# Prompt attention: the value products of a tile as two double bursts in its fifth and seventh slots, in place of four bursts in every other slot

## The chip, the cores and the metric

The kernel runs on one core of a Trainium2 chip. The metric is device microseconds of one execution, median of three runs. The core's engines work side by side and wait for each other at semaphores: TensorE (PE, matmuls and transposes into PSUM), VectorE (DVE), ScalarE (ACT), GpSimd (POOL) and the queue of SyncE (SP) that issues the transfers.

## The reference

A trunk of two encoder layers, applied to a prompt of 1024 positions and a sample of 256, both of width 1024. A layer normalises its input, projects it, and adds four groups of branches (attention, Fourier mixing, spatial gating, memory attention) through one output projection. The change touches the attention alone: 8 query heads, 2 key heads, 64 wide, no mask.

```python
def one_block(qblk):     # 128 queries
    s = jnp.einsum('bqkgd,bskd->bkgqs', qblk, k, preferred_element_type=jnp.float32) * scale
    p = jax.nn.softmax(s, axis=-1)
    return jnp.einsum('bkgqs,bskd->bqkgd', p.astype(v.dtype), v)
o_att = self_attention(q, k, v) * jax.nn.silu(ag)
```

## The kernel before

All matrix work is done in float32 or, split into a high and a low part, as float32r products. Per layer the stages follow each other: spatial gating, Fourier mixing, memory attention, the projections of queries, keys and values, then `attention` (lines 712 to 891), then `output`. The order of TensorE's instructions in the attention is that of the program; those of the other engines are ordered by a scheduler.

`attention` goes over ten tiles of 128 queries, eight of the prompt (t = 0 to 7, 1024 keys) and two of the sample (256 keys). A tile has eight slots, i = 0 to 7, called first to eighth here, one for each head, in the order 2, 0, 3, 1, 6, 4, 7, 5. So slots one, three, five and seven have the heads with j = 2 or 3 of their key head, and the even-numbered slots those with j = 0 or 1. In a slot TensorE gets, in this order:

- the score of the next slot's head (`score`, L761: four matmuls of 512 columns into an `s` tile of PSUM, of which there are two). VectorE takes the maximum (L764), ScalarE the exponential with its sum (L766). The score of a tile's first head is so issued in the eighth slot of the tile before; it is called the opening score.
- in slots one, three, five and seven the first entry of `todo`, work left by the tile before.
- in slots four and six the transposes of the next tile's queries (`turn_q`, L733, copied by ScalarE at L734).
- for heads with j below 2 the transposes of the slot's probabilities (`turn`, L794: two halves of four, copied by ScalarE at L799 into `pt`). Heads with j of 2 or 3 are transposed in blocks of 32 by VectorE instead (L776), and moved into `pd` by POOL and 12 transfers (L785, L787); for those heads TensorE gets nothing here.

The values of a tile come one tile late. `values(t, part, kts)` (lines 819 to 836) multiplies the values of some key tiles with the transposed probabilities and adds up in one PSUM tile `acc` of the pool `mm` (four buffers): part 0 for the heads that came through TensorE (`pt`), part 1 for the others (`pd`). A call for four key tiles is eight instructions of 256 columns, a burst; each has two records in the trace. `norm_gate` (L816) spreads the reciprocal row sums by four transposes and multiplies the gate by them (L817), and `finish` (L841, L842) multiplies the sum by the gate and stores it. `todo` (lines 881 to 886) says which of these goes into which slot: one burst in each of the slots one, three, five and seven, the gate's transposes behind the second, `finish` behind the last.

`pt` and `pd` are two of the four buffers `a16`. In the sample tiles one output product (`product`, L928, twelve matmuls of 512 columns) follows each slot. Its left operand is loaded, and converted by ScalarE (L915) and VectorE (L916), in `load_o`, into `a16` buffers that prompt attention gives back.

Of the kernel before, what the change touches and what calls it, by code (L numbers as in the profile page):

```python
# [74 lines left out]
def trunk_kernel(  # L75
# [10 lines left out]
    nc = tc.nc  # L86
# [29 lines left out]
    def mm(shape, dt=F32):  # L116
        return ps.tile(shape, dt, tag="mm", bufs=4, name=uid("mm_"))
# [594 lines left out]
    def attention(l, q_d, kT, v8, v2, ag, o_att):  # L712
# [5 lines left out]
        def load_q(t):  # L718
            if t < NT:
                raw[t] = c2([P, 8, HD])  # L720
                nc.sync.dma_start(raw[t], q_d[t])

        def prep_q(t):
            q = raw.pop(t)
            qhl = c4([P, 8, 2, HD], F32R)
            nc.scalar.copy(qhl[:, :, 0, :], q)
            nc.gpsimd.tensor_tensor(qhl[:, :, 1, :], q, fv(qhl)[:, :, 0, :], ALU.subtract)
            return qhl

        def turn_q(qhl, qT, kv):  # L730
            pt = mm([P, 4, P], F32R)
            for j in range(4):
                nc.tensor.transpose(pt[:, j, :], qhl[:, 4 * kv + j].rearrange("p a d -> p (a d)"), ident_r)  # L733
            nc.scalar.copy(qT[:, 4 * kv:4 * kv + 4], fv(pt))  # L734
# [3 lines left out]
        def open_tile(t):  # L738
            e = dict(prompt=t < 8, nk=SEQ if t < 8 else DEC, qT=c4([P, 8, P], F32R),
                     rs=st([P, 4, 2], tag="rowsum", bufs=3))  # L740
            tiles[t] = e

        def open_rest(t):
            e = tiles[t]
            if e["prompt"]:
                e["pt"] = a16([P, 8, 2, 2, P], F32)
                e["pd"] = a16([P, 4, 2, 8, 2, 32], F32)
            else:
                e["pt"] = [c4([P, 2, 4, P]) for _ in range(2)]

        def score(t, h):
            g, _ = group_of(t)
            e = tiles[t]
            nk = e["nk"]
            kv, j = h // 4, h % 4
            s = s2([P, 1024])
            for kg in ((0, 1) if g < 2 else (2,)):
                n = GROUPS[kg][1]
                c0 = GROUPS[kg][0] if g < 2 else 0
                for b in range(2):  # L760
                    nc.tensor.matmul(s[:, c0:c0 + n], e["qT"][:, h, :], kT[kg][b][:, kv, :],  # L761
                                     start=b == 0, stop=b == 1)
            nm = st([P, 1])
            nc.vector.tensor_reduce(nm, s[:, :nk], axis=AX.X, op=ALU.max, negate=True)  # L764
            p = c4([P, 1024])
            nc.scalar.activation(p[:, :nk], s[:, :nk], AF.Exp, bias=nm, accum_out=e["rs"][:, j, kv:kv + 1])  # L766
            e[h] = p

        def turn(t, h):
            e = tiles[t]  # L770
            kv, j = h // 4, h % 4
            p = e.pop(h)
            if e["prompt"] and j >= 2:
                if j == 2:
                    e["blocks"] = a8([P, 4, 8, 2, 32], F32)
                nc.vector.transpose(e["blocks"][:, :, :, j - 2].rearrange("p b k q -> p k b q"),  # L776
                                    p.rearrange("p (k b q) -> p k b q", b=4, q=32))
                if j == 3:
                    for r in range(4):
                        for a in range(4):  # L780
                            b = (a + r) % 4
                            dst = e["pd"][32 * b:32 * b + 32, a, kv].rearrange("p k j q -> p (k j q)")
                            src = e["blocks"][32 * a:32 * a + 32, b].rearrange("p k j q -> p (k j q)")
                            if r == 0:
                                nc.gpsimd.tensor_copy(dst, src)  # L785
                            else:
                                nc.sync.dma_start(dst, src)  # L787
                return
            for half in range(2 if e["prompt"] else 1):
                kn = 4 if e["prompt"] else 2  # L790
                pt = mm([P, 4, P])
                for kk in range(kn):
                    c0 = (half * 4 + kk) * P
                    nc.tensor.transpose(pt[:, kk, :], p[:, c0:c0 + P], ident)  # L794
                if e["prompt"]:
                    dst = e["pt"][:, half * 4:half * 4 + kn, kv, j, :]
                else:
                    dst = e["pt"][kv][:, :, j, :]
                nc.scalar.copy(dst, pt[:, :kn])  # L799

        def load_gate(t):
            gt = tiles[t]["gt"] = c2([P, 4, P])
            nc.sync.dma_start(gt, ag[t])

        def norm_rows(t):
            e = tiles[t]
            r = st([P, 4, 2], tag="rowsum_r", bufs=2)
            nc.vector.reciprocal(r, e["rs"])
            e["rb"] = c2([P, 4, 2, HD])
            nc.gpsimd.tensor_copy(e["rb"], r.unsqueeze(3).to_broadcast([P, 4, 2, HD]))  # L810

        def norm_gate(t):
            e = tiles[t]
            rt = mm([P, 4, P])
            for j in range(4):
                nc.tensor.transpose(rt[:, j, :], e["rb"][:, j].rearrange("p a d -> p (a d)"), ident)  # L816
            nc.vector.tensor_tensor(e["gt"], e["gt"], rt, ALU.mult)  # L817

        def values(t, part, kts):
            e = tiles[t]  # L820
            if "acc" not in e:
                e["acc"] = mm([P, 4, P])
            acc = e["acc"]
            last = e["nk"] // P - 1
            for kt in kts:
                for kv in range(2):
                    out = acc[kv * HD:(kv + 1) * HD]
                    vt = (v8 if t < 8 else v2)[:, kt, kv * HD:(kv + 1) * HD]
                    if not e["prompt"]:
                        out, src = out.rearrange("p j t -> p (j t)"), e["pt"][kv][:, kt].rearrange("p j t -> p (j t)")  # L830
                    elif part == 0:
                        out, src = out[:, 0:2].rearrange("p j t -> p (j t)"), e["pt"][:, kt, kv].rearrange("p j t -> p (j t)")
                    else:
                        out = out[:, 2:4].rearrange("p j (a q) -> p j a q", q=32)
                        src = e["pd"][:, :, kv, kt].rearrange("p a j q -> p j a q")
                    nc.tensor.matmul(out, vt, src, start=kt == 0, stop=kt == last)  # L836

        def finish(t):
            e = tiles.pop(t)
            o = c2([P, 4, P])  # L840
            nc.vector.tensor_tensor(o, e["acc"], e["gt"], ALU.mult)  # L841
            nc.sync.dma_start(o_att[:, :, t * P:(t + 1) * P], o)  # L842
# [13 lines left out]
        todo = []  # L856
        for n, (t, i, h) in enumerate(work):
            if i == 1 and t + 1 < NT:
                qhl = prep_q(t + 1)
            if i == 3 and t + 1 < NT:  # L860
                load_q(t + 2)
                open_tile(t + 1)
            if i == 4:
                load_gate(t)
            if i == 7 and t + 1 < NT:
                open_rest(t + 1)
            if n + 1 < len(work):
                score(work[n + 1][0], work[n + 1][2])
            if i % 2 == 0 and todo:
                for f in todo.pop(0):  # L870
                    f()
            if i in (3, 5) and t + 1 < NT:
                turn_q(qhl, tiles[t + 1]["qT"], (i - 3) // 2)
            turn(t, h)
            if i == 7:
                for fs in todo:
                    for f in fs:
                        f()
                norm_rows(t)
                if t < 8:  # L880
                    todo = [[lambda t=t, part=part, k=k: values(t, part, range(k, k + 4))]
                            for part in range(2) for k in range(0, 8, 4)]
                    todo[1].append(lambda t=t: norm_gate(t))
                else:
                    todo = [[lambda t=t: norm_gate(t)], [lambda t=t: values(t, 0, range(2))]]
                todo[-1].append(lambda t=t: finish(t))
            yield t, i
# [133 lines left out]
    for l in range(DEPTH):  # L1021
# [34 lines left out]
        last = l == DEPTH - 1  # L1056
        out_hT = []
        out = output(l, o_d, xin if l == 0 else xmid, xout if last else xmid, out_hT)
# [100 lines left out]
```

## Time and profile before

| | us |
|---|---|
| median of 3 runs | 2187.02 (2184.76 to 2191.01) |
| profiled execution | 2190.76 |
| its span, first to last instruction | 2189.0 |
| TensorE busy | 2140.2 (98%) |
| TensorE weight loads busy | 1832.7 (84%) |
| VectorE busy | 1122.5 (51%) |
| ScalarE busy | 853.1 (39%) |
| value products L836, busy | 127.9 in 1024 records |
| scores L761, busy | 163.5 in 576 records |

Busy time of TensorE is modelled, with matmuls overlapping in its pipeline, so one instruction's duration in a timeline is longer than the distance to the start of the next. In what follows distances from start to start are used. An idle time in square brackets in a timeline is that before the first instruction of the row, with what ended it.

### The profile page before, as it was taken

To read this page: it belongs to the slowest core of one execution; us is meant where nothing else is said; L and a number is where in the kernel's file an instruction comes from. 1 tells how busy PE (TensorE), PEld (TensorE's weight loads), DVE (VectorE), ACT (ScalarE), POOL (GpSimd) and SP (SyncE) were. 2 spreads that over 40 slices of the span, in tenths; PEclk is the share of its full clock that TensorE was granted. 3 is DMA by queue.
4 is the path that set the end of the run, shared out by engine and by line. 5 is a ranking of instruction groups with operands and counts; after the bars stand their busy time and mean duration, and the time that the engine had idled before them with its cause. 6 is when DMAs were issued, how large, how long until landed. Compare 5 with 4: busy or idle time off the path is not lost.

```text
span 2189.0 us, 33399 instructions
## 1 busy us (share of the span) xinstructions
PE 2140.2 (98%) x12872; PEld 1832.7 (84%) x12872; DVE 1122.5 (51%) x1972; ACT 853.1 (39%) x1935; POOL 324.7 (15%) x544
## 2 busy tenths in 40 slices
PE   7999999999999999999999999999999999999997
PEld 7898988888899777678888988888889877767885
DVE  5345344444574577534465343454557467752445
ACT  6133232333341577642254222233433267763121
POOL 2010000000032233100053000000003123310005
PEclk9999999999999999999999999999999999999999
DMA  4123431211212344522343120121112234452224
GB/s 176 57 98 116 140 109 63 71 61 35 77 50 89 108 113 118 149 86 88 106 143 113 58 78 32 63 86 48 50 63 69 80 101 124 112 151 82 87 106 144
DMA packets 113679, 202.55 MB, mean 93 GB/s; under 512 B 17393, under 2 KB 52593, under 8 KB 113521
## 3 DMA queue, kind: packets, MB, share of 16 engines
q1 hardware_dynamic: 113520, 200.42, 29.1%
q8 instruction: 102, 1.67, 0.3%
q14 instruction: 57, 0.46, 0.1%
HBM read 129.05 MB, written 46.14 MB: 80 GB/s over the span
## 4 chain that ended last, share of the span: by engine, by line
PE 87%; DMA 3%; DVE 3%; ACT 3%; POOL 2%; issue 2%; SPq 1%; DVEq 0%; POOLq 0%; ACTq 0%
PE mm L248 35%; PE mm L928 16%; PE mm L261 12%; PE s L761 6%; PE mm L836 5%; PE mm L794 3%; PE mm L311 2%; PE mm L327 1%; PE s L422 1%; PE s L408 1%; PE s L576 1%; PE mm L609 1%; POOL c L953 1%; PE s L217 1%; DVE c L961 1%
## 5 line engine op out<-in xcount | busy, mean ns | idle before, releaser
L248 PE MATMUL mm<-a,ws 128*128 128x512 f32 (+1 forms) x4032 | 795.1, 355 | 0.0
L248 PEld LDWEIGHTS mm<-a,ws 128*128 128x128 f32 x4032 | 663.6, 189 | 102.4 <-issue 0.5
L928 PE MATMUL mm<-ws,a 128*128 128x512 f32 x1632 | 381.4, 392 | 0.7 <-ACT c L935 0.6
L928 PEld LDWEIGHTS mm<-ws,a 128*128 128x128 f32 x1632 | 304.8, 188 | 65.3 <-issue 1.6
L261 PE MATMUL mm<-ws,a 128*128 128x256 f32 x2400 | 304.2, 287 | 0.0
L261 PEld LDWEIGHTS mm<-ws,a 128*128 128x128 f32 x2400 | 296.8, 195 | 0.5 <-DVE a L234 0.2
L764 DVE TENSOR_REDUCE st<-s 128x1 f32<-128x1024 f32 (+1 forms) x160 | 170.0, 1062 | 123.2 <-PE s L761 123.2
L273 ACT ACTIVATE c<-mm 128x512 f32<-128x512 f32 (+1 forms) x96 | 50.8, 529 | 322.7 <-PE mm L248 319.0
L766 ACT ACTIVATE c<-s,st 128x1024 f32<-128x1024 f32 (+1 forms) x160 | 159.2, 995 | 37.3 <-DVE st L764 36.5
L274 DVE SCALAR_TENSOR_TENSOR c<-c,mm 128x512 f32<-128x512 f32 (+1 forms) x96 | 57.3, 597 | 219.2 <-ACT c L273 219.2
L761 PE MATMUL s<-c,c 128*128 128x512 f32 (+1 forms) x576 | 163.5, 401 | 3.5 <-ACT c L766 2.8
L148 POOL TENSOR_SCALAR st<-st 128x1 f32<-128x1 f32 (+3 forms) x120 | 27.0, 225 | 745.7 <-DVE st L654 454.8
L166 ACT ACTIVATE ws<-wr,pre_g 128x256 fp32r<-128x256 f32 x304 | 126.6, 505 | 22.1 <-DMA wr<-in_w_in_dram 15.6
L836 PE MATMUL mm<-a,c 128*64 128x256 f32 x1024 | 127.9, 389 | 5.2 <-ACT a L799 5.2
L167 DVE SCALAR_TENSOR_TENSOR ws<-wr,pre_g,ws 128x256 fp32r<-128x256 f32 x304 | 128.7, 484 | 2.1 <-ACT ws L166 2.0
L761 PEld LDWEIGHTS s<-c,c 128*128 128x128 f32 x576 | 98.8, 189 | 35.0 <-issue 15.4
L937 DVE TENSOR_TENSOR c<-c,mm 128x512 f32<-128x512 f32 x120 | 81.1, 683 | 83.0 <-PE mm L928 82.9
L836 PEld LDWEIGHTS mm<-a,c 128*64 128x64 f32 x1024 | 68.8, 137 | 55.7 <-issue 19.7
L785 POOL COPY a<-a 32x512 f32<-32x512 f32 x128 | 80.2, 627 | 199.1 <-DVE a L776 141.7
L150 POOL TENSOR_TENSOR st<-st,mhalf 128x1 f32<-128x1 f32 (+3 forms) x120 | 99.8, 832 | 9.9
L953 POOL TENSOR_TENSOR c<-c,c 128x512 f32<-128x512 f32 x40 | 55.8, 1395 | 272.8 <-ACT c L948 272.7
L144 DVE TENSOR_TENSOR ws<-wr,ws 128x1024 fp32r<-128x1024 f32 x48 | 57.0, 1222 | 62.2 <-ACT ws L143 62.1
(121 smaller groups left out, 2286.0 us busy)
## 6 DMA issues: line engine op xcount, KB each, us to landing
wr<-in_w_in_dram SPq DMA_DIRECT2D x76, 512.0 KB, 4.1
a<-a SPq DMA_DIRECT2D x384, 64.0 KB, 2.0
wr<-in_w_out_dram SPq DMA_DIRECT2D x32, 512.0 KB, 3.9
wr<-o SPq DMA_DIRECT2D x48, 256.0 KB, 3.0
c<-in_x_prompt_dram SPq DMA_DIRECT2D x16, 512.0 KB, 6.4
o<-c SPq DMA_DIRECT2D x32, 256.0 KB, 2.0
wr<-in_w_mem_kv_dram SPq DMA_DIRECT2D x16, 512.0 KB, 4.5
q<-c SPq DMA_DIRECT2D x40, 128.0 KB, 1.7
```

Of the source, the lines that this page charges most:

```text
L150: nc.gpsimd.tensor_tensor(r, m, mhalf[:, :n], ALU.pow)
L166: nc.scalar.activation(w[:, 0, kk], raw[:, k], AF.Copy, scale=g)
L167: nc.vector.scalar_tensor_tensor(w[:, 1, kk], raw[:, k], g, fv(w)[:, 0, kk], ALU.mult, ALU.subtract)
L248: nc.tensor.matmul(acc[:, :n], w[:, a, k, c * P:(c + 1) * P], hT.t[g][b][:, k, :], start=i == 0, stop=i == 3 * KC - 1)
L261: nc.tensor.matmul(acc[:, :256], hT.t[g][a][:, k, tt * P:(tt + 1) * P], w[:, b, k, :], start=i == 0, stop=i == 3 * KC - 1)
L761: nc.tensor.matmul(s[:, c0:c0 + n], e["qT"][:, h, :], kT[kg][b][:, kv, :], start=b == 0, stop=b == 1)
L764: nc.vector.tensor_reduce(nm, s[:, :nk], axis=AX.X, op=ALU.max, negate=True)
L766: nc.scalar.activation(p[:, :nk], s[:, :nk], AF.Exp, bias=nm, accum_out=e["rs"][:, j, kv:kv + 1])
L785: nc.gpsimd.tensor_copy(dst, src)
L836: nc.tensor.matmul(out, vt, src, start=kt == 0, stop=kt == last)
L928: nc.tensor.matmul(acc, oT[g][c][:, a, tt * P:(tt + 1) * P], w[:, b, c, :], start=j == 0, stop=j == 11)
L937: nc.vector.tensor_tensor(ys, ys, acc, ALU.add)
```

## The change

The list `todo` that a prompt tile leaves for the next has an empty entry for the first slot, the gate's transposes for the third, and for the fifth and the seventh a burst of part 0 and one of part 1 for the same four key tiles. As both parts now begin in one slot and share the PSUM tile, only the first matmuls of part 0 carry the start flag, and only the last of part 1 (or of part 0 in a sample tile) the stop flag.

```diff
-                    nc.tensor.matmul(out, vt, src, start=kt == 0, stop=kt == last)
+                    nc.tensor.matmul(out, vt, src, start=kt == 0 and part == 0, stop=kt == last and part == int(e["prompt"]))
...
                 if t < 8:
-                    todo = [[lambda t=t, part=part, k=k: values(t, part, range(k, k + 4))]
-                            for part in range(2) for k in range(0, 8, 4)]
-                    todo[1].append(lambda t=t: norm_gate(t))
+                    todo = [[], [lambda t=t: norm_gate(t)]]
+                    todo += [[lambda t=t, part=part, k=k: values(t, part, range(k, k + 4)) for part in range(2)]
+                             for k in range(0, 8, 4)]
```

TensorE, first layer, second prompt tile, first to third slot. Names: `s` are scores, `mm` PSUM tiles of the other kinds, `a` the transposed probabilities. Before:

```order
L836 MATMUL mm_7406<-a_925_7073,c_698_5348 64x256 x8
L761 MATMUL s_989_7420<-c_693_5343,c_950_7243 128x512
L761 MATMUL s_989_7420<-c_694_5344,c_950_7243 128x512
L761 MATMUL s_989_7420<-c_695_5345,c_950_7243 128x512
L761 MATMUL s_989_7420<-c_696_5346,c_950_7243 128x512
L794 MATMUL mm_7429<-ident,c_985_7404 128x128 x4
L794 MATMUL mm_7435<-ident,c_985_7404 128x128 x4
L761 MATMUL s_994_7441<-c_693_5343,c_950_7243 128x512
L761 MATMUL s_994_7441<-c_694_5344,c_950_7243 128x512
L761 MATMUL s_994_7441<-c_695_5345,c_950_7243 128x512
L761 MATMUL s_994_7441<-c_696_5346,c_950_7243 128x512
L836 MATMUL mm_7406<-a_925_7073,c_698_5348 64x256 x8
```

After:

```order
L761 MATMUL s_988_7411<-c_693_5343,c_950_7243 128x512
L761 MATMUL s_988_7411<-c_694_5344,c_950_7243 128x512
L761 MATMUL s_988_7411<-c_695_5345,c_950_7243 128x512
L761 MATMUL s_988_7411<-c_696_5346,c_950_7243 128x512
L794 MATMUL mm_7420<-ident,c_985_7404 128x128 x4
L794 MATMUL mm_7426<-ident,c_985_7404 128x128 x4
L761 MATMUL s_993_7432<-c_693_5343,c_950_7243 128x512
L761 MATMUL s_993_7432<-c_694_5344,c_950_7243 128x512
L761 MATMUL s_993_7432<-c_695_5345,c_950_7243 128x512
L761 MATMUL s_993_7432<-c_696_5346,c_950_7243 128x512
L816 MATMUL mm_7441<-ident,c_982_7395 128x128 x4
```

The two bursts are gone from these slots, and only scores, one pair of transpose halves and the gate's transposes are left.

TensorE, the same tile, fifth slot. Before:

```order
L761 MATMUL s_1008_7514<-c_693_5343,c_950_7243 128x512
L761 MATMUL s_1008_7514<-c_694_5344,c_950_7243 128x512
L761 MATMUL s_1008_7514<-c_695_5345,c_950_7243 128x512
L761 MATMUL s_1008_7514<-c_696_5346,c_950_7243 128x512
L836 MATMUL mm_7406<-a_926_7074,c_698_5348 64x256 x8
L761 MATMUL s_1012_7533<-c_693_5343,c_950_7243 128x512
```

The same slot after:

```order
L761 MATMUL s_1007_7497<-c_693_5343,c_950_7243 128x512
L761 MATMUL s_1007_7497<-c_694_5344,c_950_7243 128x512
L761 MATMUL s_1007_7497<-c_695_5345,c_950_7243 128x512
L761 MATMUL s_1007_7497<-c_696_5346,c_950_7243 128x512
L836 MATMUL mm_7506<-a_925_7073,c_698_5348 64x256 x8
L836 MATMUL mm_7506<-a_926_7074,c_698_5348 64x256 x8
L761 MATMUL s_1012_7525<-c_693_5343,c_950_7243 128x512
```

The slot now has a burst of `pt` (a_925) ahead of that of `pd` (a_926).

ScalarE, first layer, from the last two exponentials of the last prompt tile (128x1024) to those of the first sample tile (128x256); `wr` is loaded attention output, L915 its conversion. Before:

```order
L766 ACTIVATE c_1302_8902,st_8619<-s_1300_8895,st_8900 128x1024
L766 ACTIVATE c_1308_8929,st_8619<-s_1306_8922,st_8927 128x1024
L915 ACTIVATE a_1330_9034<-wr_9035 128x256
L915 ACTIVATE a_1327_9019<-wr_9020 128x512 x2
L915 ACTIVATE a_1327_9019<-wr_9027 128x512 x2
L915 ACTIVATE a_1330_9034<-wr_9035 128x256
L799 COPY a_1262_8732<-mm_8968 128x4x128
L766 ACTIVATE c_1314_8966,st_8846<-s_1312_8961,st_8964 128x256
```

The same stretch after:

```order
L766 ACTIVATE c_1302_8894,st_8602<-s_1300_8887,st_8892 128x1024
L766 ACTIVATE c_1308_8921,st_8602<-s_1306_8914,st_8919 128x1024
L915 ACTIVATE a_1323_8995<-wr_8996 128x512 x2
L915 ACTIVATE a_1323_8995<-wr_9003 128x512 x2
L915 ACTIVATE a_1326_9010<-wr_9011 128x512 x2
L799 COPY a_1262_8732<-mm_8968 128x4x128
L799 COPY a_1262_8732<-mm_8974 128x4x128
L766 ACTIVATE c_1314_8966,st_8829<-s_1312_8961,st_8964 128x256
```

The conversions of the first operand (a_1323, before a_1324 and in the middle of the last prompt tile) now stand behind that tile's last exponential, with two of the second; the rest of the second and the third follow later.

## Rows read from the trace of the kernel before

**Rows 1.** The page, busy us of each engine, share of the span, instructions.

```profile
PE 2140.2 (98%) x12872; PEld 1832.7 (84%) x12872; DVE 1122.5 (51%) x1972; ACT 853.1 (39%) x1935; POOL 324.7 (15%) x544
```

**Rows 2.** Timeline of TensorE, one prompt tile: start us, us, engine, line, out<-in, count.

```profile
771.06 1.20 PE L761 MATMUL s<-c,c 128*128 128x512 f32 x4
772.10 1.03 PE L794 MATMUL mm<-ident,c 128*128 128x128 f32 x8
772.89 1.17 PE L761 MATMUL s<-c,c 128*128 128x512 f32 x4
773.98 1.95 PE L836 MATMUL mm<-a,c 128*64 128x256 f32 x16
775.86 1.19 PE L761 MATMUL s<-c,c 128*128 128x512 f32 x4
...
780.66 0.66 PE L816 MATMUL mm<-ident,c 128*128 128x128 f32 x4
781.07 1.18 PE L761 MATMUL s<-c,c 128*128 128x512 f32 x4
782.08 0.46 PE L733 MATMUL mm<-ident_r,c 128*128 128x128 f32 x4
782.38 1.06 PE L794 MATMUL mm<-ident,c 128*128 128x128 f32 x8
...
791.31 1.20 PE L761 MATMUL s<-c,c 128*128 128x512 f32 x4
```

**Rows 3.** Timelines of VectorE and ScalarE in the same tile.

```profile
774.09 1.22 DVE L764 TENSOR_REDUCE st<-s 128x1 f32<-128x1024 f32 x1 [0.57 <-PE s L761]
775.23 1.23 DVE L776 STREAM_TRANSPOSE a<-c 128x1024 f32<-128x1024 f32 x1
...
772.73 1.07 ACT L799 COPY a<-mm 128x512 f32<-128x512 f32 x2 [0.91 <-PE mm L794]
...
775.41 1.12 ACT L766 ACTIVATE c<-s,st 128x1024 f32<-128x1024 f32 x1 [0.50 <-DVE st L764]
776.42 0.19 ACT L766 ACTIVATION_READ_ACCUMULATOR c<-s,st 128x1 f32 x1
```

**Rows 4.** Timelines of TensorE and ScalarE, last slots of the first prompt tile.

```profile
747.67 1.17 PE L761 MATMUL s<-c,c 128*128 128x512 f32 x4
750.26 1.20 PE L761 MATMUL s<-c,c 128*128 128x512 f32 x4 [1.42 <-ACT c L766]
751.78 1.09 PE L794 MATMUL mm<-ident,c 128*128 128x128 f32 x8 [0.32 <-ACT c L766]
752.63 1.17 PE L761 MATMUL s<-c,c 128*128 128x512 f32 x4
...
748.97 1.15 ACT L766 ACTIVATE c<-s,st 128x1024 f32<-128x1024 f32 x1
...
750.52 1.12 ACT L766 ACTIVATE c<-s,st 128x1024 f32<-128x1024 f32 x1 [0.32 <-DVE st L764]
```

**Rows 5.** Timelines of TensorE and ScalarE, last prompt tile and first sample tile.

```profile
872.39 1.20 PE L761 MATMUL s<-c,c 128*128 128x512 f32 x4
...
893.78 0.50 PE L761 MATMUL s<-c,c 128*128 128x256 f32 x2
...
898.84 3.26 PE L836 MATMUL mm<-a,c 128*64 128x256 f32 x14 [2.40 <-ACT a L799]
...
902.37 3.15 PE L928 MATMUL mm<-ws,a 128*128 128x512 f32 x12
...
882.65 2.18 ACT L915 ACTIVATE a<-wr 128x512 fp32r<-128x512 f32 x4
```

**Rows 6.** Windows: stretch, us, busy of each engine (records), granted clock, DMA share, GB/s.

```profile
744.00:757.00 13.00, 11.26 (x68) 8.20 (x68) 7.95 (x9) 8.25 (x15) 3.13 (x6) 1.00 0.45 121
...
899.00:903.00 4.00, 4.00 (x18) 2.31 (x17) 1.20 (x3) 1.43 (x6) 0.00 (x0) 0.57 0.38 86
```

## The prediction

> **What bounds the kernel now.** I read the page's busy table first, then TensorE's timeline of one prompt tile, then the timelines of VectorE and ScalarE beside it, then the places where TensorE does wait. The table shows TensorE busy 2140.2 us of the span [rows 1]: whatever changes the time must change TensorE's work or its waits. The tile timeline [rows 2] shows which of the two it can be. From the score at 771.06 to the same score of the next tile at 791.31 are 20.25 us, and no row between has an idle time before it: in the prompt tiles TensorE is the bound and ScalarE and VectorE only follow. Start to start, a score (four matmuls, L761) takes 1.04 us before transposes and 1.09 before a burst; the eight transposes (L794) 0.79; a burst (L836, eight instructions, sixteen records) 1.88; the gate's transposes (L816) 0.41; the query's (L733) 0.30.
>
> Behind each score hangs a chain, which [rows 3] price: score start to maximum start 1.20 us (772.89 to 774.09); maximum start to exponential start 1.32 (774.09 to 775.41); and 1.14 from one VectorE instruction to the next. Transposes are followed 0.63 us later by their two copies on ScalarE (772.10 to 772.73), 1.07 long. From exponential start to the transposes that wait for it are 1.26 us (750.52 to 751.78) and to the score that waits for its PSUM buffer 1.29 (748.97 to 750.26) [rows 4]. So a score's buffer is free some 3.8 us after the score began, and there are two such buffers: score n+2 cannot start before exponential n is done. The bursts in slots one, three, five and seven are what TensorE does meanwhile. [rows 4] are the one place in prompt attention where such a slot now has neither burst nor other work in its stead (the first tile's last two slots): the score at 750.26 waits 1.42 us and the transposes 0.32. That pair of slots took 4.96 us (747.67 to 752.63), while a pair with a burst takes 4.80 (771.06 to 775.86): the missing 1.88 us were not saved at all.
>
> **The change, step by step.** The 32 value instructions of a tile stay, with the same shapes; the start and stop flags alone cost nothing, as the count of TensorE instructions is the same (6881 in the order before and after). What moves is their place: slots one and three lose a burst, slots five and seven get a double one of 3.76 us. Without waits a tile would gain a little, since two scores more are followed by something else than a burst, 1.04 in place of 1.09: 2 x 0.05 = 0.1 us, 20.15 in all.
>
> The waits I work out from these durations, with zero at the opening score (the one at 771.06 in the old order); scores and exponentials are counted by their place in the tile, from 0. Transposes of the old tile 1.04, score 1 at 1.83, TensorE free at 2.87. Exponential 0: maximum at 1.20 gives 2.52, but ScalarE copies the old tile's transposes from 1.67 to 2.63; so it starts at 2.6 and releases its buffer at 3.9. **Score 2 waits 1.0 us**, to 3.9. Exponential 1 starts at 4.35 (score 1.83, maximum 3.03), ends for TensorE at 5.6, when TensorE has been free since 4.9: **transposes 1 wait 0.7.** Score 3 at 6.4, gate transposes 7.4, free 7.85. Maximum 2 cannot start at 5.1, because VectorE is in the block transposes (L776) of exponential 0 until 5.3; and ScalarE is in the copies of transposes 1 from 6.2 to 7.2; exponential 2 at 7.2, release 8.5: **score 4 waits 0.6.** Query transposes 9.5; exponential 3 (score 6.4, maximum 7.6, exponential 8.9) ends at 10.2: **transposes 3 wait 0.4.** Score 5 at 11.0. From here nothing waits: 1.09 and 3.76 of burst, score 6 at 15.8, 2.13 with the query's and the head's transposes, score 7 at 17.96, 1.09 and 3.76, next opening score at 22.8. The waits are 2.7 us, the two cheaper scores 0.1: 22.81 - 20.25, **2.56 us more a tile.** Bounds: below, if every one of the four links is 0.2 us shorter than its row, 1.8; above, the pair in [rows 4], where two slots without a burst cost 4.96 against 4.80 - 1.88 = 2.92 of TensorE's own work, that is 2.0 a pair and 4.0 a tile, less 0.1. I take the working, because its links are rows of the same instructions in the same neighbourhood; the pair has gate work on ScalarE that the later tiles lack.
>
> Seven of the eight prompt tiles of a layer carry the bursts of the tile before. Six of them get 2.56. The last one takes 21.39 us now (872.39 to 893.78 [rows 5]), because four conversions for the output projection (L915, 2.18 us at 882.65) sit on ScalarE between its exponentials. Those conversions write buffers that hold the transposed probabilities of the tile before; the first of them is free at the end of the burst of slot three now, and of slot seven after the change, so the order shows them behind exponential 7. That tile then takes the 22.8 of the others: 1.4 more.
>
> **First sample tile.** Now the opening score is at 893.78, the first burst waits 2.40 us and then crawls (14 records in 3.26 us), and the first output product (L928) starts at 902.37 [rows 5]: 8.59 us, of which 1.88 are the burst. After the change the first slot has no burst; six conversions of about 0.55 us (four took 2.18) start when exponential 7 is done, 1.1 us before the opening score, and end 2.2 after it; copies to 3.2, the short exponential to about 3.8, then transposes and the product at about 4.1. That gains 8.59 - 1.88 - 4.1 = 2.6 us. Against it stand an idle time of 2 us in a row, which may let the clock fall, and the loads of the other half of the converted data, which are now issued behind the attention store and seven block copies. Bounds: 3.5 gained, 3 lost; I take 2.0 gained a layer, near the worked figure.
>
> What is hidden: the store of the attention output is queued four block copies later on SP, and the last eight of those copies go out behind it; they end some 7 us into the tile and are wanted at 12. The buffers of the transposed probabilities are written again 6 us after their last burst. VectorE's product with the gate (L841) swaps places with a reciprocal; both are done before the next maximum.
>
> **Sum:** two layers of 6 x 2.56 + 1.4 - 2.0 = 14.8 us, 29.5 us. On the profiled execution's 2190.76 us that is 2220.3. That execution lies 3.74 us above the median of 2187.02, so the median to expect is **2216.5 us**, 1.35% slower. About 0.3% (6.6 us) is what a measurement of this kernel can tell from no change.
>
> **Rivals.**
> *The clock falls as well (0.18).* After the idle 2.40 us before 898.84 the granted clock was 0.57 in the four microseconds from 899, the 1.2 GHz level for most of them; in the stretch from 744 to 757, with idle 1.42 and 0.32 us, it stayed at 1.00 [rows 6]. The longest single wait I expect is 1.0 us, under the harmless one, but there are four in some 8 us. One fall costs 1.6 us at most (14 records took 3.26 in place of 14/16 of 1.88, 1.64), so 14 tiles up to 22 us more: 2238 us if it happens in each. The Trainium skill (TensorE: Matmul & The Clock Gate, A second HAM failure mode) says that frequent short idles of TensorE between groups of matmuls, while it cycles through PSUM buffers, can make its clock swing between the two levels. By that rule this kernel would land here; [rows 4] and [rows 6] speak against it so far, with one such pair a layer and a full clock.
> *The output product is late in the first sample tile (0.06).* If the loads behind the store hold up ScalarE, the copies of the products wait too: 3 us lost a layer in place of 2.0 gained, 2226 us.
> *TensorE stays the bound (0.04).* If the two score buffers bridged the empty slots, only the two cheaper scores and the first sample tile would remain: 14 x 0.1 + 2 x 2.6 = 6.6 us off, up to 2 x 3.5 + 1.4 = 8.4, 2180 us, faster. It decides at one point: exponential 0 would have to release its buffer at 2.87 after the opening score, not 3.9, that is a chain 1.0 us shorter. The wait of 1.42 in [rows 4] speaks against it.
> *Half of that (0.04).* With waits of 0.6 us a tile the gain in the first sample tile nearly cancels them: 12 x (0.6 - 0.1) - 4 = 2 us, within 0.3%. The same row speaks against it.
>
> **How the numbers follow.** The forecast has 0.68. Its own range, from 1.8 to 3.2 us (halfway to the pair's figure) in the 12 tiles and from 3.5 gained to 3 lost in the first sample tile, is about 2204 to 2234; the clock's part reaches beyond to 2240. I give 2204 to 2240. Slower by over 0.3% is the forecast, the clock and the late product: 0.92; within 0.3% 0.04; faster 0.04.
>
> **What would show it.** In the changed profile a prompt tile should take 22.8 us from one opening score to the next, with TensorE idle in the second and fourth slots only, all put down to ScalarE's L766: in the second before a score and before transposes, in the fourth likewise. The trace counts idle time from a matmul's modelled end, which is 1.2 us after a score's start and not 1.04, so it should show about 0.9, 0.5, 0.4 and 0.2. The double bursts should be 3.8 us and unbroken. The granted clock in the tiles should stay at 1.00. The first output product should come about 4 us after the score that opens the first sample tile. I am wrong if a tile takes 20.3 us or less, if the waits sit in the double bursts (probabilities or block copies late), or if the clock falls in the tiles.

## The result and the profile after

| | before, us | after, us |
|---|---|---|
| median of 4 runs | 2187.40 (2184.76 to 2191.01) | 2214.97 (2213.16 to 2219.17) |
| profiled execution, its span | 2190.76, 2189.0 | 2213.52, 2211.7 |
| the seven prompt tiles of the first layer that carry value products of the tile before | 143.52 | 159.20 |
| its sample tiles, from their opening score to the second tile's value products | 70.67 | 68.47 |

The ratio is 1.0128 [1.0112, 1.0145]: 27.6 us slower between the medians. The two profiled executions lie only 22.8 us apart, since the one before is above its median and the one after below; the stages that the change touches are therefore compared by their own rows, not by the spans. What the spans differ by outside the attention is told behind the tiles.

The page of the kernel after, busy us of each engine, and two of its costliest groups (line, engine, operation, shapes, count | busy us, mean ns of one | idle us before it and what ended it).

```profile
PE 2136.4 (97%) x12872; PEld 1831.6 (83%) x12872; DVE 1122.7 (51%) x1972; ACT 852.9 (39%) x1935; POOL 323.7 (15%) x544
...
L761 PE MATMUL s<-c,c 128*128 128x512 f32 (+1 forms) x576 | 164.0, 402 | 23.3 <-ACT c L766 22.7
...
L794 PE MATMUL mm<-ident,c 128*128 128x128 f32 x576 | 81.3, 277 | 14.7 <-ACT c L766 14.7
```

The same two groups in the kernel before.

```profile
L761 PE MATMUL s<-c,c 128*128 128x512 f32 (+1 forms) x576 | 163.5, 401 | 3.5 <-ACT c L766 2.8 <-ACT c L734 0.7
...
L794 PE MATMUL mm<-ident,c 128*128 128x128 f32 x576 | 81.0, 276 | 2.5 <-ACT c L766 1.9 <-DVE c L817 0.6
```

Beside [rows 1]: the counts are the same, and every engine has as much work as before. TensorE is even 3.8 us less busy in a longer span. What is new is idle time: 38.0 us ahead of scores and transposes (3.5 and 2.5 before), nearly all ended by ScalarE's exponential L766; the 5.2 us that the bursts L836 waited before are gone. That is 38.0 - 6.0 - 5.2 = 26.8 us more idle and 3.8 less busy, 23.0 in all, against 22.7 between the two spans.

The timeline of TensorE in one prompt tile after (start us, us, engine, line, out<-in, count, idle before the first).

```profile
793.77 1.20 PE L761 MATMUL s<-c,c 128*128 128x512 f32 x4
...
795.60 1.18 PE L761 MATMUL s<-c,c 128*128 128x512 f32 x4
797.68 1.20 PE L761 MATMUL s<-c,c 128*128 128x512 f32 x4 [0.90 <-ACT c L766]
799.39 1.09 PE L794 MATMUL mm<-ident,c 128*128 128x128 f32 x8 [0.51 <-ACT c L766]
...
802.38 1.19 PE L761 MATMUL s<-c,c 128*128 128x512 f32 x4 [0.52 <-ACT c L766]
...
804.03 1.09 PE L794 MATMUL mm<-ident,c 128*128 128x128 f32 x8 [0.17 <-ACT c L766]
...
805.98 3.67 PE L836 MATMUL mm<-a,c 128*64 128x256 f32 x32
809.59 1.20 PE L761 MATMUL s<-c,c 128*128 128x512 f32 x4
...
816.45 1.20 PE L761 MATMUL s<-c,c 128*128 128x512 f32 x4
```

Opening score to opening score is 22.67 us (793.77 to 816.45), where [rows 2] have 20.25 without a wait. The four waits sit in the second and the fourth slot, and nowhere else: the fifth to the eighth slot run without a gap, and the double burst is one unbroken row of 32 records.

What the first of them waits for, from the timelines of VectorE and ScalarE in the same slot.

```profile
795.01 1.23 DVE L764 TENSOR_REDUCE st<-s 128x1 f32<-128x1024 f32 x1 [0.43 <-PE s L761]
...
795.45 1.08 ACT L799 COPY a<-mm 128x512 f32<-128x512 f32 x2 [2.65 <-PE mm L794]
796.41 1.13 ACT L766 ACTIVATE c<-s,st 128x1024 f32<-128x1024 f32 x1
```

From the score at 793.77 to its maximum are 1.24 us, to the exponential behind the copies another 1.40, and 1.27 from there to the score at 797.68, which takes the freed buffer: 3.91 us. TensorE was done with its own work at 796.64 (795.60 and 1.04 of a score).

The tiles of the layer add up as follows. The first one that carries bursts took 23.15 us (before 20.80), the next five 22.67 (20.25), the last prompt tile 22.68 (21.39): 2.35 + 5 x 2.42 + 1.29 = 15.7 us lost. The sample tiles give 2.2 us back. That is 13.5 us a layer; layer two lost 15.71 in its prompt tiles and got back 2.19. Twice 13.5 are 27.0 of the 27.6 us. The two spans differ by 4.3 us less, since the profiled execution before was slower outside the attention: from its start to the first score 716.14 us against 713.83, and from the second sample tile's value products to the first score of layer two 784.86 against 782.88. TensorE's granted clock fell there three times before (0.67 from 594.9 to 600 us, 0.66 from 1161 to 1166 and from 1629 to 1634), and not at all after.

The first sample tile: timelines of TensorE and ScalarE, then the windows of its first output product and of the seven prompt tiles ahead of it (us, busy of each engine with records, granted clock, DMA share, GB/s).

```profile
907.15 0.51 PE L761 MATMUL s<-c,c 128*128 128x256 f32 x2
...
910.77 0.44 PE L794 MATMUL mm<-ident,c 128*128 128x128 f32 x2 [2.00 <-ACT c L766]
910.96 4.58 PE L928 MATMUL mm<-ws,a 128*128 128x512 f32 x12
...
975.62 1.94 PE L836 MATMUL mm<-c,c 128*64 128x512 f32 x8
...
906.08 3.22 ACT L915 ACTIVATE a<-wr 128x512 fp32r<-128x512 f32 x6
...
911.00:915.00 4.00, 4.00 (x13) 3.15 (x12) 1.60 (x3) 0.83 (x3) 0.13 (x1) 0.58 0.44 106
...
747.95:907.15 159.20, 144.21 (x981) 101.70 (x981) 110.75 (x108) 107.31 (x194) 48.35 (x72) 1.00 0.42 105
```

The six conversions start 1.07 us before the opening score and end 2.15 after it; behind them come the copies and the exponential, and TensorE idles 2.00 us. The product starts 3.81 us after the opening score, where it took 8.59 with a burst in between [rows 5]. In its window the granted clock is 0.58, near the 1.2 GHz level. Over the seven prompt tiles, with four waits each, it is 1.00, and over those of layer two (1792.63 to 1951.81) as well.

### The profile page after: what moved, and what is told of

Same layout as the page of the kernel before. It is cut to its first block, busy times and chain, and to the rows that moved or that the text cites. A ratio compares the mean times of both kernels' runs of the same rounds, so it can differ in the third digit from the quotient of the medians.

```text
span 2211.7 us, 33395 instructions
## 1 busy us (share of the span) xinstructions
PE 2136.4 (97%) x12872; PEld 1831.6 (83%) x12872; DVE 1122.7 (51%) x1972; ACT 852.9 (39%) x1935; POOL 323.7 (15%) x544
## 4 chain that ended last, share of the span: by engine, by line
PE 86%; DVE 4%; ACT 3%; DMA 3%; issue 2%; POOL 1%; SPq 0%; DVEq 0%; ACTq 0%; POOLq 0%
PE mm L248 34%; PE mm L928 16%; PE mm L261 12%; PE mm L836 5%; PE s L761 4%; PE mm L794 3%; PE mm L311 2%; DVE st L764 2%; PE mm L327 1%; PE s L422 1%; PE s L408 1%; PE s L576 1%; ACT c L766 1%; PE mm L609 1%; PE s L217 1%
## 5 line engine op out<-in xcount | busy, mean ns | idle before, releaser
L261 PE MATMUL mm<-ws,a 128*128 128x256 f32 x2400 | 299.2, 285 | 0.0
L761 PE MATMUL s<-c,c 128*128 128x512 f32 (+1 forms) x576 | 164.0, 402 | 23.3 <-ACT c L766 22.7
L766 ACT ACTIVATE c<-s,st 128x1024 f32<-128x1024 f32 (+1 forms) x160 | 159.4, 996 | 35.6 <-DVE st L764 35.0
L836 PE MATMUL mm<-a,c 128*64 128x256 f32 x1024 | 117.6, 382 | 0.0
L836 PEld LDWEIGHTS mm<-a,c 128*64 128x64 f32 x1024 | 70.7, 137 | 43.0 <-issue 10.1
L794 PE MATMUL mm<-ident,c 128*128 128x128 f32 x576 | 81.3, 277 | 14.7 <-ACT c L766 14.7
```

Source lines behind the costliest of these rows:

```text
L261: nc.tensor.matmul(acc[:, :256], hT.t[g][a][:, k, tt * P:(tt + 1) * P], w[:, b, k, :], start=i == 0, stop=i == 3 * KC - 1)
L836: nc.tensor.matmul(out, vt, src, start=kt == 0 and part == 0, stop=kt == last and part == int(e["prompt"]))
```

## The experiments

The theory: with two score buffers, a pair of scores can go no faster than the chain through maximum and exponential; a slot without a burst makes TensorE wait for that chain, and a burst that was moved costs its full time again where it lands. The rivals: the flags, the double bursts themselves, the clock, or the place of the waits matter. Diffs are against the changed kernel unless they say otherwise.

### The flags alone

The order of before, with the start and stop flags of the change; against the kernel before only this line differs.

```diff
-                    nc.tensor.matmul(out, vt, src, start=kt == 0, stop=kt == last)
+                    nc.tensor.matmul(out, vt, src, start=kt == 0 and part == 0, stop=kt == last and part == int(e["prompt"]))
```

> The order of before with the start and stop flags of the change. Theory (empty slots let the chain from score to released score buffer show): the flags have no price; a prompt tile stays at 20.25 us and the time at 2187, within 0.3%. Rival (the two parts share one accumulation and wait for each other in PSUM): the tile grows, up to the whole 2.4 us of the change, and the time goes towards 2215.

Measured: 2188.43 us, 1.0002 [0.9992, 1.0011] of before; a prompt tile is 20.25 to 20.27 us. One tile is not: the first that carries bursts in layer one takes 22.37 us (20.80 before), and the granted clock was 0.57 there from 752 to 756 us. In layer two the same tile takes 20.80, so this is the clock and not the flags (see the last section). The flags cost nothing. The whole loss belongs to the order. (The two profiles have 12872 records of TensorE each; the count of 6881 that the prediction gives stands in no trace.)

### One empty slot in place of two

One burst in the first slot, two in the fifth, one in the seventh; only the third is without.

```diff
-                    todo = [[], [lambda t=t: norm_gate(t)]]
-                    todo += [[lambda t=t, part=part, k=k: values(t, part, range(k, k + 4)) for part in range(2)]
-                             for k in range(0, 8, 4)]
+                    v = [lambda t=t, part=part, k=k: values(t, part, range(k, k + 4))
+                         for part in range(2) for k in range(0, 8, 4)]
+                    todo = [[v[0]], [lambda t=t: norm_gate(t)], [v[1], v[2]], [v[3]]]
```

> One burst in slots one and seven, two in slot five, the gate's transposes alone in slot three. Theory: only the fourth slot waits, about 0.5 us before its score and 0.7 before its transposes by the trace's count; tile 21.5 us (21.2 to 21.9), time 2203 (2197 to 2210), with the first sample tile as in before. Rival (the double burst itself is what costs, as ScalarE and VectorE run dry behind it): waits follow the double burst in slots five and six; tile near 21.4 too, so the place of the waits decides, not the sum.

Measured: 2201.10 us, 1.0064 [1.0049, 1.0079]. TensorE's timeline of one prompt tile:

```profile
794.82 1.20 PE L761 MATMUL s<-c,c 128*128 128x512 f32 x4
...
803.57 1.19 PE L761 MATMUL s<-c,c 128*128 128x512 f32 x4 [0.51 <-ACT c L766]
...
805.25 1.09 PE L794 MATMUL mm<-ident,c 128*128 128x128 f32 x8 [0.18 <-ACT c L766]
...
815.93 1.20 PE L761 MATMUL s<-c,c 128*128 128x512 f32 x4
```

The tile takes 21.11 us, 0.86 more than before, with two waits only, both in the fourth slot, equal to the fourth-slot pair of the change to 0.01 us. The second slot, which has its burst ahead of it again, has none. So each empty slot brings its own pair of waits, and the double burst in the fifth slot none. The tile was expected at 21.5 us (21.2 at the least): the wait ahead of the transposes had been put at 0.7 us and is 0.18. That the time still lies in its range is partly luck, since the sample tiles, expected as before, took 72.18 and 71.41 us in place of 70.67 and 70.59.

### The same two double bursts in other slots

Two bursts in the first slot and two in the fifth, none in the third and the seventh.

```diff
-                    todo = [[], [lambda t=t: norm_gate(t)]]
-                    todo += [[lambda t=t, part=part, k=k: values(t, part, range(k, k + 4)) for part in range(2)]
-                             for k in range(0, 8, 4)]
+                    v = [lambda t=t, part=part, k=k: values(t, part, range(k, k + 4))
+                         for part in range(2) for k in range(0, 8, 4)]
+                    todo = [[v[0], v[1]], [lambda t=t: norm_gate(t)], [v[2], v[3]]]
```

> Two double bursts as in the change, but spread: in slots one and five, slots three and seven without. Theory: two slots without a burst each let the chain show once, and nothing is gained by the even distance; waits in the fourth slot and in the seventh to eighth slots, tile 23.3 us (22.8 to 23.6), time 2228 (2218 to 2238). Rival (the unevenness between the halves of the tile is the cost, ScalarE's load in one half): an even spread brings the tile back to 20.2 to 21, time 2187 to 2197.

Measured: 2223.63 us, 1.0165 [1.0148, 1.0182]. The timeline from one score of the sixth slot to the next:

```profile
813.46 1.20 PE L761 MATMUL s<-c,c 128*128 128x512 f32 x4
...
817.71 1.20 PE L761 MATMUL s<-c,c 128*128 128x512 f32 x4 [0.93 <-ACT c L766]
819.39 1.09 PE L794 MATMUL mm<-ident,c 128*128 128x128 f32 x8 [0.49 <-ACT c L766]
...
828.90 1.19 PE L761 MATMUL s<-c,c 128*128 128x512 f32 x4 [0.52 <-ACT c L766]
...
830.57 1.09 PE L794 MATMUL mm<-ident,c 128*128 128x128 f32 x8 [0.17 <-ACT c L766]
...
836.13 1.20 PE L761 MATMUL s<-c,c 128*128 128x512 f32 x4
```

The period is 22.67 us, that of the change. The waits have moved behind the slots that are empty now, the eighth and the fourth, and kept their sizes. The tile had been expected longer, at 23.3 us (22.8 at the least), with the second pair of waits in the seventh and eighth slots; the time, expected at 2228, lies in its range. In the prompt tiles it does not matter which two slots are empty, nor that they lie apart: the seven of the first layer take 159.20 us, as in the change. That this kernel is 8.7 us slower than the change comes from the sample tiles: from their opening score to the second tile's value products they take 73.28 us (909.06 to 982.34), where the change takes 68.47, and 71.36 against 68.40 in layer two. In the first layer's the clock fell twice (0.58 from 913 to 917 us, 0.57 from 947 to 951), in the change once; where the rest of the loss comes from, no run shows.

### Useless bursts in the empty slots

The change, with one burst of eight instructions in the first slot and one in the third that write a buffer nobody reads.

```diff
+        def fill(t):
+            e = tiles[t]
+            x = mm([P, 4, P])
+            for kt in range(4):
+                for kv in range(2):
+                    nc.tensor.matmul(x[kv * HD:(kv + 1) * HD, 0:2].rearrange("p j t -> p (j t)"), v8[:, kt, kv * HD:(kv + 1) * HD],
+                                     e["pt"][:, kt, kv].rearrange("p j t -> p (j t)"), start=kt == 0, stop=kt == 3)
...
-                    todo = [[], [lambda t=t: norm_gate(t)]]
+                    todo = [[lambda t=t: fill(t)], [lambda t=t: fill(t), lambda t=t: norm_gate(t)]]
```

> The change, with one burst of eight value instructions more in each of slots one and three, whose sums go to a PSUM tile that nothing reads. Theory: the waits in slots two and four vanish, as they are cover that is missing; the tile goes from 22.67 to 23.8 us, that is 1.1 us more for 3.7 us of added TensorE work; time 2236 (2228 to 2243). Rival (TensorE is still the bound, or the waits have another cause): the added work is paid in full, tile 26.3, time 2265 to 2273.

Measured: 2233.86 us, 1.0212 [1.0197, 1.0228]. TensorE's timeline (L843 are the added bursts):

```profile
798.13 1.20 PE L761 MATMUL s<-c,c 128*128 128x512 f32 x4
...
801.06 1.95 PE L843 MATMUL mm<-a,c 128*64 128x256 f32 x16
...
805.86 1.95 PE L843 MATMUL mm<-a,c 128*64 128x256 f32 x16
...
821.85 1.20 PE L761 MATMUL s<-c,c 128*128 128x512 f32 x4
```

The tile takes 23.72 us (23.8 was expected) and has no wait at all. Two bursts of 1.88 us are 3.76 us of work more, and the tile is only 1.05 longer: the other 2.7 us stood there as waits. This is the sum of waits that the prediction worked out (2.7), measured from the other side.

### A shorter link in the chain, in the change and in the kernel before

The maximum reads 256 of the 1024 columns, and the queries are scaled down so that the exponentials stay small; the output of both kernels is therefore another one. The first kernel is the change with this edit, the second the kernel before with it (and with the old order and flags).

```diff
-    tabq = rope_tables(l, q_g, q_gs, HD ** -0.5)
+    tabq = rope_tables(l, q_g, q_gs, HD ** -0.5 / 64)
...
-            nc.vector.tensor_reduce(nm, s[:, :nk], axis=AX.X, op=ALU.max, negate=True)
+            nc.vector.tensor_reduce(nm, s[:, :256], axis=AX.X, op=ALU.max, negate=True)
```

> The change with the maximum taken over 256 of the 1024 columns, 0.41 us in place of 1.23, and queries scaled by 1/64 so that the exponentials stay finite; the output is another one. The chain from a score to its released buffer is 0.8 us shorter, ScalarE's work the same; the scheduler also puts two block transposes and some copies of VectorE and ScalarE at other places, among them a block transpose ahead of the last maximum of the first half. Theory (the length of the chain sets the waits): worked out with that order, waits of 0.6, 0.5 and 0.9 us in place of 1.0, 0.7, 0.6 and 0.4, tile 22.1 us (21.6 to 22.4), time 2208 (2202 to 2212). Rival (ScalarE's throughput, 15.0 us of each tile, sets them): tile 22.67, time 2215. Rival (the maximum alone is the bound): tile 20.3, time 2187.

> The same short maximum and scale in the order of before, as a control. All theories: TensorE has no wait in the middle tiles, so they stay at 20.25 us; time 2187, or up to 5 us less from the last prompt tile, where VectorE is crowded.

Measured: the change with it 2200.36 us, 1.0052 [1.0037, 1.0068] of before; the kernel before with it 2188.42, 1.0004 [0.9994, 1.0013]. The timeline of TensorE in the first, and what its first score runs through:

```profile
792.89 1.20 PE L761 MATMUL s<-c,c 128*128 128x512 f32 x4
...
794.12 0.42 DVE L764 TENSOR_REDUCE st<-s 128x1 f32<-128x256 f32 x1 [0.43 <-PE s L761]
...
794.56 0.58 ACT L799 COPY a<-mm 128x512 f32<-128x512 f32 x1 [2.42 <-PE mm L794]
...
795.04 1.12 ACT L766 ACTIVATE c<-s,st 128x1024 f32<-128x1024 f32 x1
...
796.31 1.19 PE L761 MATMUL s<-c,c 128*128 128x512 f32 x4 [0.41 <-ACT c L766]
...
797.89 1.09 PE L794 MATMUL mm<-ident,c 128*128 128x128 f32 x8 [0.39 <-ACT c L766]
...
802.39 1.09 PE L794 MATMUL mm<-ident,c 128*128 128x128 f32 x8 [0.80 <-ACT c L766]
...
814.81 1.20 PE L761 MATMUL s<-c,c 128*128 128x512 f32 x4
```

One prompt tile of the second kernel.

```profile
790.22 1.20 PE L761 MATMUL s<-c,c 128*128 128x512 f32 x4
...
810.53 1.20 PE L761 MATMUL s<-c,c 128*128 128x512 f32 x4
```

The maximum is 0.8 us shorter (0.42 against 1.23), and the chain 3.42 us (792.89 to 796.31) against 3.91. It is not the full 0.8 shorter because the exponential still stands behind one of the old tile's copies on ScalarE. The tile falls from 22.67 to 21.92 us; expected was 22.1. The time came out 1.6 us below its range: the first prompt tile got shorter too (32.66 us against 34.12), and the first output products take 3.02 and 2.99 us in place of 4.58 in both layers.

In the kernel before the same edit leaves the middle tiles without a wait, at 20.31 us, and the time where it was. It is not without effect there: the first and the last prompt tile are shorter (32.66 against 34.12, 20.31 against 21.39), the sample tiles longer (73.96 and 71.25 against 70.67 and 70.59), and the sum cancels. In a middle tile the two orders are now 21.92 - 20.31 = 1.61 us apart, where they were 2.42 apart with the whole maximum: 0.81 less, which is what the maximum lost. So the chain bounds the changed kernel's tiles and did not bound the old ones': what the change did was to make a maximum count that had been covered.

### The new places in the last prompt tile's work alone

Only the values of t = 7, done in the first sample tile, get the new places.

```diff
-                if t < 8:
+                if t < 7:
+                    todo = [[lambda t=t, part=part, k=k: values(t, part, range(k, k + 4))]
+                            for part in range(2) for k in range(0, 8, 4)]
+                    todo[1].append(lambda t=t: norm_gate(t))
+                elif t == 7:
```

> The new places for the last prompt tile alone, whose values fall into the first sample tile; the other seven keep the places of before. Theory: the prompt tiles stay at 20.25 us, the last at 21.4; in the first sample tile the burst that waited 2.4 us is gone, and output products cover the empty slots, which gains 1 to 3 us a layer, so 2183 us (2180 to 2186), 0.1 to 0.3% faster than before. Rival (the gain seen in the first sample tile comes from the conversions, which here stay in the middle of the last prompt tile): no gain there, 2187.

Measured: 2190.61 us, 1.0010 [1.0002, 1.0019]: no gain, where 2183 (2180 to 2186) was expected. Timelines of TensorE and ScalarE:

```profile
892.69 0.50 PE L761 MATMUL s<-c,c 128*128 128x256 f32 x2
...
898.18 0.44 PE L794 MATMUL mm<-ident,c 128*128 128x128 f32 x2 [3.41 <-ACT c L766]
898.38 4.58 PE L932 MATMUL mm<-ws,a 128*128 128x512 f32 x12
...
894.39 2.80 ACT L919 ACTIVATE a<-wr 128x256 fp32r<-128x256 f32 x6 [1.01 <-DMA wr<-o]
```

The product does come 5.69 us after the opening score (8.59 before), but TensorE idles 3.41 us ahead of it and the product takes 4.58 us. From the opening score to the second sample tile's value products are 70.58 us, as before (70.67). The conversions (L919 in this kernel, the products L932) still stand ahead of the copies, and six of them start 1.70 us after the opening score, when a transfer has landed, as they did before (1.73 us, 895.51). The empty first slot alone gains nothing.

### The last two prompt tiles' work

The new places for t = 6 and t = 7.

```diff
-                if t < 8:
+                if t < 6:
+                    todo = [[lambda t=t, part=part, k=k: values(t, part, range(k, k + 4))]
+                            for part in range(2) for k in range(0, 8, 4)]
+                    todo[1].append(lambda t=t: norm_gate(t))
+                elif t < 8:
```

> The new places for the last two prompt tiles: the last prompt tile carries its values in slots five and seven, so the conversions for the output projection move behind it as in the change; the six tiles before keep the places of before. Theory now (the gain of the first sample tiles comes with the conversions' new place, not with the empty first slot): last prompt tile 22.7 us in place of 21.4, the two sample tiles 68.5 us from the opening score to the second tile's value products in place of 70.6, as in the change; net 0.9 us a layer less, time 2186, 0.1% under before, hardly to be told from no change. Rival (the gain needs the waits of the earlier tiles): sample tiles at 70.6, time 2190.

Measured: 2186.62 us, 0.9996 [0.9988, 1.0005]. TensorE at the first sample tile of both layers, with the windows of their products:

```profile
897.30 4.57 PE L932 MATMUL mm<-ws,a 128*128 128x512 f32 x12
...
898.00:902.00 4.00, 4.00 (x14) 3.18 (x13) 0.94 (x3) 0.86 (x4) 0.00 (x0) 0.57 0.37 82
...
1929.98 0.44 PE L794 MATMUL mm<-ident,c 128*128 128x128 f32 x2 [2.00 <-ACT c L766]
1930.18 2.99 PE L932 MATMUL mm<-ws,a 128*128 128x512 f32 x12
...
1930.00:1934.00 4.00, 4.00 (x21) 3.41 (x22) 2.24 (x4) 1.56 (x5) 0.34 (x1) 1.00 0.59 152
```

With the bursts of t = 6 moved as well the sample tiles take 68.39 us, as in the change. The last prompt tile takes 22.67 in place of 21.39. The first layer is 1.0 us shorter from that tile's opening score (91.06 against 92.06), too little to measure over two layers. In layer two the sample tiles took 66.97 us: there the same idle 2.00 us was not followed by a lower clock, and the product took 2.99 us in place of 4.57. So the gain of the change in the first sample tile comes with the conversions' place, which hangs on the bursts done in the last prompt tile; no run moves the conversions alone, so that they are its cause is argued and not shown. No version that was run beats the kernel before by more than its measurement tells.

## Why the prediction was right

The forecast was 2216.5 us, the median is 2214.97; the case that it gave 0.68 is the one that happened. By its steps:

**Which resource bounds a pair of slots.** Right, and shown. TensorE's busy time says nothing of it: it fell. Filling the empty slots took all waits away; shortening the maximum shortened the tile in the change alone.

**The waits.** Worked out as 1.0, 0.7, 0.6 and 0.4 us, traced as 0.90, 0.51, 0.52 and 0.17 where 0.9, 0.5, 0.4 and 0.2 were announced, all put down to L766. The buffer was released 3.91 us after the opening score; 3.9 was worked out. The working from four links held; they were rows of the same instructions, and the copies and the block transposes that stand between them on ScalarE and VectorE were counted in.

**The double burst: mis-sized.** It was taken as two bursts, 3.76 us; it takes 3.61 from start to start (805.98 to 809.59). What is missing, 0.15 us each, makes 0.3 a tile. The third wait came out longer by 0.1. So, with the roundings of the working, a tile lost 2.42 us, not 2.56, and 22.67 stands for 22.81. The first of the tiles with bursts lost 2.35, the last 1.29 (1.4 said). Together 15.7 us a layer against 16.8.

**The last prompt tile's 21.39 us.** The size was right, the reason only in part. The prediction put the 1.1 us that it takes beyond the others down to the four conversions on ScalarE. With the short maximum in the order of before the four stand in the same place (2.20 us from 881.31), and the tile takes 20.31 us, like the others. So it took the full maximum as well: before, VectorE has its own part of the conversions (L916, 883.30 to 887.52) between the maximums of that tile.

**The first sample tile: near by luck.** Gained 2.2 us a layer where 2.0 was taken. The conversions started and ended where the working had them, and the product came at 3.81 us, not 4.1. The working gave 2.6 to gain before the risks; the drop of the clock that was weighed against it did come, after the idle 2.00 us, in both layers. It made the product 4.58 us long where 2.99 is its length at full clock: 1.6 us lost. In the last experiment's second layer, without that drop, 3.6 us were gained (66.97 against 70.59). So the worked gain was 1.0 too small, and the fall, which had been weighed but had no term of its own, took 1.4 of the 3.6 away over the two tiles. The 2.0 was a choice between bounds, and the two errors nearly cancel.

**Sum.** 15.7 - 2.2 = 13.5 us a layer in place of 14.8, 27.0 in place of 29.5. Against it stand 0.4 us of the base (the median before is 2187.40 with a fourth run, and the forecast used 2187.02) and 0.6 us between 27.0 and the medians' 27.6 that no row accounts for.

**The rivals.** The clock did not fall in the prompt tiles: 1.00 over all seven in both layers. The Trainium skill (TensorE: Matmul & The Clock Gate, A second HAM failure mode) tells of a kernel where it swings because TensorE idles briefly and often while it cycles through PSUM buffers. The trace does not agree here: four waits of 0.17 to 0.90 us in 22.67 us left the clock where it was. But the ground that the prediction had for it did not hold. It took the idle 1.42 and 0.32 us of [rows 4] for harmless, from one layer. The same pair stands in the first prompt tile of eight of the kernels in both layers, and in five of these sixteen places the clock fell behind it. The tiles' waits were below it; that none of them was followed by a fall was not to be read from that row. The output product was early, not late. TensorE did not stay the bound, and the loss was not near the 0.5 us a tile of the last rival: it was 2.42.

What stays open: a third score buffer would test the chain from its other end; no run has one. Why the clock fell behind some idle times and not behind others of the same length is not shown either.

## What to carry to other kernels

When two buffers stand between a producer and a chain of other engines, work for the producer between the two runs for nothing as long as the chain is the longer: taking it out of a slot saves little (here 1.05 of 3.76 us for two bursts), and where the producer is the bound it is paid nearly in full. So spread such work evenly, and before moving it compare the chain's length with what is left in the slot. Before a gain at a stage's edge is put down to the instructions moved, look at which buffer they release, and what a scheduler puts in its place.

## What the runs showed of the hardware

A double burst is 0.15 us shorter than two single ones, 3.61 against 3.76: a burst that follows another directly costs about that much less.

What an idle time does to the clock is not read from its length. The idle 2.00 us ahead of the first sample tile was followed by a granted clock of 0.57 or 0.58 in both layers of the change and in the first of the last experiment, and by 1.00 in that one's second layer, with the same instructions. In the change with the short maximum an idle 2.22 us at the same place was followed by 1.00 in both layers. In the kernel with the bursts in the first and the fifth slot an idle 1.84 us was enough:

```profile
946.04 0.44 PE L794 MATMUL mm<-ident,c 128*128 128x128 f32 x2 [1.84 <-ACT c L766]
946.24 4.58 PE L928 MATMUL mm<-ws,a 128*128 128x512 f32 x12
...
947.00:951.00 4.00, 4.00 (x13) 3.17 (x12) 1.75 (x3) 1.96 (x6) 0.61 (x1) 0.57 0.29 103
```

The product behind it takes 4.58 us, as behind 2.00.

The pair of 1.42 and 0.32 us in the first prompt tile ([rows 4]) is in the kernel before and in seven of the changed ones, with the same instructions. The granted clock behind it was 0.57 in layer one of the flags alone and of the one empty slot, in both layers of the useless bursts, and in layer two of the last experiment; in the other eleven cases it did not fall. One such fall costs 1.6 us here, whatever the idle time before it: 4.58 against 2.99 for the product, 22.37 against 20.80 for the tile. So two profiles of one kernel can differ by a few falls, and their stages are better compared than their spans.
